# Modulation weights of the feed-forward stages: scaled and summed on DVE and POOL instead of multiplied on PE

## The chip, the cores and the metric

The kernel runs on one core of a Trainium2 chip. The metric is the device time of one execution in microseconds. Five engines take part: PE (matmuls; PEld is its weight load), DVE and ACT (elementwise work), POOL (elementwise work, here also the triangular inverses), and SP, whose queue issues nearly all DMA transfers.

## The reference, cut to what matters

One inference step of a diffusion backbone with two layers. Each layer has a feed-forward half step, a stage of token mixing, and a second feed-forward half step; ahead of each stands a norm whose shift, scale and gate come from conditioning vectors.

```python
def modulation(cond, w_mod, b_mod):
    m = jax.nn.silu(cond) @ w_mod + b_mod
    return m.reshape(cond.shape[0], N_MOD, D_MODEL)      # N_MOD = 9, D_MODEL = 1024

def adaln(x, g, shift, scale):
    return rms_norm(x, g) * (1.0 + scale) + shift

def swiglu(h, w_in, w_out):
    gate, up = jnp.split(h @ w_in, 2, axis=-1)           # w_in 1024 x 5632, w_out 2816 x 1024
    return (jax.nn.silu(gate) * up) @ w_out
```

There are two conditioning vectors (context tokens and latent tokens), so the product with `w_mod` (1024 x 9216 in each layer) has two rows of input. 128 context tokens and 128 latent tokens go through the same weights.

## The kernel before

Activations lie channel-major: 128 channels on the partitions, 8 chunks of channels, 256 tokens in a row. Weights are fp32 and stream through SBUF in tiles `raw` of 128 x 1024 (three buffers). Half a tile at a time is split into two parts that sum to it, `hi` on ACT and `lo = raw - hi` on DVE (four buffers each, `split`, lines 155 and 158), and every pair of a 128 x 128 weight block and a chunk of activations takes three matmuls on PE: `hi` with the high and the low part of the activations, `lo` with the high part.

`ffn` is run four times, and is called here the first to the fourth feed-forward stage. It loops over 11 pairs of column blocks: `pg` (gate) and `pu` (up) are 48 matmuls each, out of eight halves of weight tiles; ACT, DVE and DVE again make `z` out of them, which is split into `zhi` and `zlo`. Then five output units `po` follow (three of 256 columns, two of 128), whose result is added to `xT` on DVE. After a stage comes the next norm (`adaln`, with `rstd`: `pss`, `nr`, `prs`, `u`, `hhi`, `hlo`).

A modulation vector is 1024 columns of `w_mod`, in eight row chunks `mraw` of 128 x 1024. `mod_part` makes eight loads and eight products of it, and a last step. A product is four matmuls with the chunk of the conditioning vectors `cT` (2 of 32 columns used) as the stationary operand, into four groups of partitions of one PSUM tile `acc`; the profile counts two records for each of these fp32 matmuls. The last step copies `acc` to `modrow` on ACT, transposes it with two matmuls (`acct`) and adds the bias on DVE (`mod`). Of the 18 vectors two are done at the start, six in the first feed-forward stage, four each in the second and third, and one in each mixing stage. `fill` emits loads and products up to counts that grow with the blocks of the stage; in the first three stages the last 18 steps (`KEEP`) are left to `flush`, which emits them in the following norm. A list scheduler then sets the order on each engine by priorities and its own estimates; every engine and SP's queue work strictly in that order.

Of the kernel before, what the change touches and what calls it, by code (L numbers as in the profile page):

```python
# [10 lines left out]
F32 = mybir.dt.float32  # L11
# [4 lines left out]
ALU = mybir.AluOpType  # L16
# [8 lines left out]
OUT_UNITS = ((0, 2), (2, 2), (4, 2), (6, 1), (7, 1))      # first chunk and number of chunks of the output products  # L25
# [4 lines left out]
# column offsets of w_in  # L30
# [3 lines left out]
def constants():  # L34
    """Tables that depend on shapes alone, packed along the free dimension."""
# [28 lines left out]
    for d in range(2):  # L64
        for l in (16, 8, 4, 2, 1):
            tt = (t16 // l) * 2 * l + t16 % l + (l if d == 0 else 0)      # token of a compact index
            su = (si % (2 * l)) >= l
            ms.append(f((si // (2 * l) == tt // (2 * l)) & (su if d else ~su)))
# [29 lines left out]
KEEP = (18, 18, 18, 0)  # L98
MRAW, NQ = 16, 15


class Net:
    def __init__(self, ctx, tc, ia, oa, dbg=None):
# [13 lines left out]
        self.ch = 0                 # which of the two chains of small products is being written  # L117
# [63 lines left out]
    def after(self, later, earlier):  # L181
        """issue order of two instructions of one queue"""
        self.tc.add_manual_dep(later.ins, earlier.ins.name,
                               mybir.DependencyInfo(mybir.DependencyClass.NoSync, mybir.DependencyReason.DATA),
                               reason="issue order")
# [12 lines left out]
    def wload(self, srcs, nk, nc_):  # L198
        """srcs: list of (column offset in tile, dram view [128, nk, n])."""
# [7 lines left out]
        def part(k0, n):  # L207
            """rows k0 .. k0 + n as two f32r parts that sum to them"""
# [10 lines left out]
    def gemm(self, out2, wview, nkc, xhi, xlo, ncol=256, segs=None):  # L219
        """out2: psum tile [128, 512] -> (2, 256) column chunks; weights  # L220
        stationary, channel-major activations moving."""
# [23 lines left out]
    def params_g(self):  # L245
        """conditioning vectors and modulation biases first, the small parameters later"""
# [40 lines left out]
    def mod_part(self, tiles, l, v):  # L287
        """a modulation vector (1024 columns) as loads and products, a pair per weight tile, and a
        last step. Column groups of 256 in the four column tiles of the PE array."""
# [19 lines left out]

        def last():  # L310
            row = self.sm.tile([128, 256], F32, tag="mrow", name="modrow", bufs=2)
# [4 lines left out]
            # chunk of the vector = j * 2 + c  # L316
# [6 lines left out]
        return [partial(load, k) for k in range(8)], [partial(prod, k) for k in range(8)] + [last]  # L323

    def queue(self, parts):
        """modulation work for the rest of the sublayer"""
# [5 lines left out]
        tiles = lambda: [pool.tile([128, 1024], F32, tag="mraw", name="mraw", bufs=MRAW)]  # L332
        for p in parts:
            x, y = self.mod_part(tiles, *p)
# [3 lines left out]
    def fill(self, nload, nprod):  # L338
        """the queued loads and products up to these counts, the loads never too few"""
# [5 lines left out]
    def flush(self):  # L345
        """what is left, in the shadow of a norm"""
# [5 lines left out]
    def modcols(self, l, i):  # L352
        """per-sublayer columns: g * (1 + scale), shift, gate factor."""
# [13 lines left out]
    def rsqrt(self, p, n, scale, eps):  # L367
        """(p * scale + eps)^-1/2 of [128, n]: a first guess from the exponent, then three
        Newton steps (the sign alternates)"""
# [10 lines left out]
    def rstd(self):  # L380
        """[128, 256] psum: 1 / rms of every token, on all partitions"""
# [21 lines left out]
    def headnorm(self, x, n, scale, eps):  # L403
        """(sum over each 64-partition group of x^2 * scale + eps)^-1/2: psum tiles of 512 columns of x"""
# [20 lines left out]
    def adaln(self, l, i):  # L425
        """x * g (1 + scale) ahead of the norm factor, which comes last; at the start the
        other way round, as the modulation comes last there"""
# [32 lines left out]
    def ffn(self, l, w, i):  # L460
        """the modulation parts are spread over the products; the last steps (keep) wait for the next norm"""
# [39 lines left out]
    # SBUF of this phase is shared by tag: tiles of one tag have disjoint lives.  # L501
# [29 lines left out]
    def padded(self, p):  # L531
        """[128, (2 chunks, 2 streams, 128)] psum -> sbuf with a zero column at each end"""
# [43 lines left out]
    def proj_gate(self, c0, nm):  # L576
        """x * (1 + tanh(x / 2)): silu without its factor 1/2, which is in the norm weights"""
# [8 lines left out]
    def proj_t(self, l):  # L586
        """token-major: values of B and D, the scalar gates of C"""
# [33 lines left out]
    def proj_d(self, l):  # L621
        """q with the heads in the order 0, 2 | 1, 3, and k"""
# [833 lines left out]
```

## Time and profile before

| | |
|---|---|
| median of three runs | 1675.52 us (1665.06 to 1677.17) |
| span of the profiled execution | 1665.8 us |
| busy: PE, DVE, ACT, POOL | 1620.0, 1057.8, 811.3, 143.7 us |
| feed-forward stages one to four, products only | 218.1, 203.2, 201.2, 189.0 us |
| mean granted clock of TensorE | 0.979 |

No time of the profiled execution is listed beside its span. A busy time is the time in which at least one instruction of the engine was under way. The stretch of a stage is taken from its first `pg` matmul to its last `po` matmul.

### The profile page before, as it was taken

What the parts mean: (1) busy time and instruction counts of PE and PEld (TensorE: products, weight loads), DVE (VectorE), ACT (ScalarE), POOL (GpSimd) and SP (SyncE); (2) the same over time, 40 slices, a digit from 0 to 9 for tenths busy, and PEclk for the clock granted to TensorE, in tenths of its full rate; (3) what the DMA queues carried; (4) which work ended last, traced back from release to release, by engine and by line L of the source; (5) the groups of instructions that cost most, each with busy time, mean ns of one, the idle gap of its engine ahead of it and who ended that gap; (6) DMA issues with size and microseconds to landing.
All of it is one profiled execution on the core that took longest, in us unless ns stands there. A gap on an engine that the chain in (4) does not pass through costs nothing.

```text
span 1665.8 us, 34996 instructions
## 1 busy us (share of the span) xinstructions
PE 1620.0 (97%) x13862; PEld 1465.2 (88%) x13872; DVE 1057.8 (64%) x2270; ACT 811.3 (49%) x1529; POOL 143.7 (9%) x304
## 2 busy tenths in 40 slices
PE   6999999999999999999999999999999999999997
PEld 3999988788778998999989999887887899989997
DVE  4555557667687477665566655674857774866655
ACT  3444445446444455454455545551744443655553
POOL 0000000043007000000000000000700350000000
PEclk9999999999999999999999999998989998999999
DMA  9998775344246455976669766551423563645553
GB/s 342 315 318 297 238 238 164 80 117 114 64 132 199 127 173 195 324 266 221 213 228 316 245 213 211 189 139 48 122 74 95 158 195 95 187 143 182 186 184 121
DMA packets 300821, 311.14 MB, mean 187 GB/s; under 512 B 48368, under 2 KB 278768, under 8 KB 300656
## 3 DMA queue, kind: packets, MB, share of 16 engines
q1 hardware_dynamic: 300368, 307.85, 58.2%
q8 instruction: 109, 1.79, 0.4%
q10 hardware_dynamic: 288, 1.05, 0.2%
q14 instruction: 56, 0.46, 0.1%
HBM read 303.87 MB, written 4.98 MB: 185 GB/s over the span
## 4 chain that ended last, share of the span: by engine, by line
PE 75%; DVE 4%; POOL 2%; DMA 2%; ACT 2%; issue 1%; SPq 0%; POOLq 0%; DVEq 0%; ACTq 0%
PE pg L170 20%; PE po L170 15%; PE pu L170 13%; PE wk L170 6%; PE sv L170 4%; PE pA L170 3%; PE acc L170 3%; PE pC L170 1%; PE pD L170 1%; PE yA L170 1%; PE pR L170 1%; PE pT L170 1%; POOL itmp L842 1%; POOL Tb L843 1%; DVE lo L158 1%
## 5 line engine op out<-in xcount | busy, mean ns | idle before, releaser
L158 DVE TENSOR_TENSOR lo<-raw,hi 128x512 fp32r<-128x512 f32 (+2 forms) x840 | 581.0, 696 | 394.0 <-ACT hi L155 381.8
L155 ACT ACTIVATE hi<-raw 128x512 fp32r<-128x512 f32 (+2 forms) x840 | 523.2, 626 | 592.4 <-PE pg L170 192.3
L170 PE MATMUL pg<-hhi,hi 128*128 128x256 f32 x1216 | 356.5, 293 | 6.0 <-ACT hi L155 2.9
L170 PE MATMUL pg<-hlo,hi 128*128 128x256 f32 x1216 | 352.8, 290 | 0.5 <-DVE hlo L158 0.3
L170 PE MATMUL pg<-hhi,lo 128*128 128x256 f32 x1216 | 349.7, 288 | 0.8 <-DVE lo L158 0.6
L170 PEld LDWEIGHTS pg<-hhi,hi 128*128 128x128 f32 x1216 | 236.0, 194 | 23.6 <-issue 8.8
L170 PEld LDWEIGHTS pg<-hlo,hi 128*128 128x128 f32 x1216 | 236.1, 194 | 7.7 <-issue 4.4
L170 PEld LDWEIGHTS pg<-hhi,lo 128*128 128x128 f32 x1216 | 236.7, 195 | 3.1 <-DVE lo L158 2.3
L170 PE MATMUL pu<-hhi,lo 128*128 128x256 f32 x704 | 199.3, 283 | 0.0
L170 PE MATMUL pu<-hlo,hi 128*128 128x256 f32 x704 | 199.2, 283 | 0.0
L170 PE MATMUL pu<-hhi,hi 128*128 128x256 f32 x704 | 199.2, 283 | 0.0
L170 PE MATMUL po<-zhi,hi 128*128 128x256 f32 x704 | 198.6, 282 | 0.0
L170 PE MATMUL po<-zhi,lo 128*128 128x256 f32 x704 | 196.8, 280 | 0.0
L170 PE MATMUL po<-zlo,hi 128*128 128x256 f32 x704 | 196.7, 279 | 0.0
L170 PEld LDWEIGHTS po<-zhi,hi 128*128 128x128 f32 x704 | 132.6, 188 | 6.2 <-issue 4.5
L170 PEld LDWEIGHTS pu<-hhi,lo 128*128 128x128 f32 x704 | 135.2, 192 | 0.1
L170 PEld LDWEIGHTS pu<-hhi,hi 128*128 128x128 f32 x704 | 135.2, 192 | 0.0
L170 PEld LDWEIGHTS pu<-hlo,hi 128*128 128x128 f32 x704 | 135.2, 192 | 0.0
L170 PEld LDWEIGHTS po<-zhi,lo 128*128 128x128 f32 x704 | 132.9, 189 | 0.0
L170 PEld LDWEIGHTS po<-zlo,hi 128*128 128x128 f32 x704 | 132.5, 188 | 0.0
L170 PE MATMUL acc<-mraw,cT 128*32 128x256 f32 x1152 | 85.7, 403 | 9.6 <-DMA mraw<-in_w_mod 9.5
L191 POOL COPY GB<-SA 32x128 f32<-32x128 f32 x16 | 5.7, 355 | 911.2 <-DMA out_o_v<-VD 584.6
(354 smaller groups left out, 2610.6 us busy)
## 6 DMA issues: line engine op xcount, KB each, us to landing
raw<-in_ffn_w_in SPq DMA_DIRECT2D x176, 512.0 KB, 4.5
mraw<-in_w_mod SPq DMA_DIRECT2D x138, 512.0 KB, 5.7
raw<-in_w_in SPq DMA_DIRECT2D x106, 512.0 KB, 3.6
raw<-in_ffn_w_out SPq DMA_DIRECT2D x76, 512.0 KB, 4.4
raw<-in_w_branch SPq DMA_DIRECT2D x32, 256.0 KB, 3.2
raw<-in_w_out SPq DMA_DIRECT2D x16, 512.0 KB, 4.1
raw<-in_ffn_w_out SPq DMA_DIRECT2D x12, 256.0 KB, 3.0
raw<-in_ffn_w_out SPq DMA_DIRECT2D x8, 384.0 KB, 4.4
```

Source lines behind the costliest of these rows:

```text
L155: self.nc.scalar.activation(out, in_, func, bias=bias, scale=scale, **kw)
L158: self.nc.vector.tensor_tensor(out, a, b, op)
L170: self.nc.tensor.matmul(out, lhsT, rhs, start=start, stop=stop)
L191: (self.nc.vector if eng == "v" else self.nc.gpsimd).tensor_copy(out, in_)
L842: nc.gpsimd.tensor_tensor(tv, a, b, ALU.mult)
L843: nc.gpsimd.tensor_tensor(T[:, 0:n, j + 1:32], T[:, 0:n, j + 1:32], tv, ALU.subtract)
```

## The change

In the three feed-forward stages that carry modulation work, a chunk of weights no longer goes to PE. Each chunk is multiplied with the two conditioning values of its rows (a scalar for each partition) and added to two running sums `macc` of 128 x 1024, one for each conditioning vector: the second sum on DVE with one instruction a chunk, the first on POOL with two, of which the first overwrites the chunk. When all eight chunks are added, PE sums the 128 rows of both with a matmul against a column of ones (`sel`), into the same layout as before, and the last step goes on as it was. The two vectors at the start and the two of the mixing stages keep their products. `KEEP` falls from 18 to 1, the buffers of `mraw` from 16 to 10, and four buffers `macc` are added.

```diff
-KEEP = (18, 18, 18, 0)
-MRAW, NQ = 16, 15
+KEEP = (1, 1, 1, 0)
+MRAW, MACC, NQ = 10, 4, 15
...
+        self.sel = self.cp.tile([128, 2, 32], F32, name="sel")
+        nc.gpsimd.memset(self.sel, 0.0)
+        for e in range(2):
+            nc.gpsimd.memset(self.sel[:, e, e:e + 1], 1.0)
...
-    def mod_part(self, tiles, l, v):
+    def mod_part(self, tiles, l, v, sums=None):
...
+        def fold(k):
+            raw, = raws.pop(k)
+            if k == 0:
+                acc.extend([sums(), sums()])
+            c0, c1 = [self.cT[:, k, e:e + 1] for e in range(2)]
+            if k == 0:
+                self.ts(acc[1], raw, c1, None, ALU.mult)
+                self.nc.gpsimd.tensor_scalar(acc[0], raw, c0, None, ALU.mult)
+            else:
+                self.stt(acc[1], raw, c1, acc[1], ALU.mult, ALU.add)
+                self.nc.gpsimd.tensor_scalar(raw, raw, c0, None, ALU.mult)
+                self.nc.gpsimd.tensor_tensor(acc[0], acc[0], raw, ALU.add)
+
+        def rows():
+            p = self.py.tile([128, 256], F32, tag="y", name="acc")
+            for e in range(2):
+                for j in range(4):
+                    self.mm(p[32 * j:32 * j + 32], self.sel[:, e], acc[e][:, 256 * j:256 * j + 256], e == 0, e == 1)
+            acc[:] = [p]
+
         def last():
+            if sums:
+                rows()
...
-        return [partial(load, k) for k in range(8)], [partial(prod, k) for k in range(8)] + [last]
+        step = fold if sums else prod
+        return [partial(load, k) for k in range(8)], [partial(step, k) for k in range(8)] + [last]
...
-        tiles = lambda: [pool.tile([128, 1024], F32, tag="mraw", name="mraw", bufs=MRAW)]
+        tiles = lambda: [pool.tile([128, 1024], F32, tag="mraw", name="mraw", bufs=MRAW if fold else 16)]
+        sums = lambda: pool.tile([128, 1024], F32, tag="macc", name="macc", bufs=MACC)
...
-        net.queue([(0, 0), (0, 1)])
+        net.queue([(0, 0), (0, 1)], False)
```

On DVE, early in the first stage, the stream before has only the residuals and the work on `z`:

```order
L158 TENSOR_TENSOR zlo<-z,zhi 128x512
L158 TENSOR_TENSOR lo<-raw,hi 128x512 x4
L161 SCALAR_TENSOR_TENSOR z<-z,pg 128x512
L158 TENSOR_TENSOR lo<-raw,hi 128x512 x3
L158 TENSOR_TENSOR z<-z,pu 128x512
```

and after the change the sums stand among them, one by one or up to three in a row:

```order
L161 SCALAR_TENSOR_TENSOR z<-z,pg 128x512
L161 SCALAR_TENSOR_TENSOR macc<-mraw,cT,macc 128x1024 x3
L158 TENSOR_TENSOR z<-z,pu 128x512
L158 TENSOR_TENSOR lo<-raw,hi 128x512 x2
L158 TENSOR_TENSOR zlo<-z,zhi 128x512
L158 TENSOR_TENSOR lo<-raw,hi 128x512 x4
L161 SCALAR_TENSOR_TENSOR macc<-mraw,cT,macc 128x1024
L158 TENSOR_TENSOR lo<-raw,hi 128x512 x2
```

What moved: nothing of the old work; 112 instructions of 1024 columns were put in between.

POOL, which had no work in these stages, now has the following from the first chunk of the first vector on (the tile numbers tell the chunks apart; DMAHW is a transfer, and a wait for DVE is one for DVE's reading of the chunk):

```order
L324 TENSOR_SCALAR macc_496<-mraw_490,cT_102 128x1024 [waits DMAHW1_49,DVE_49]
L327 TENSOR_SCALAR mraw_492<-mraw_492,cT_102 128x1024 [waits DMAHW2_49,DVE_49]
L328 TENSOR_TENSOR macc_496<-macc_496,mraw_492 128x1024 [waits Pool_49]
L327 TENSOR_SCALAR mraw_494<-mraw_494,cT_102 128x1024 [waits DMAHW4_49,DVE_49]
L328 TENSOR_TENSOR macc_496<-macc_496,mraw_494 128x1024 [waits Pool_49]
```

Each chunk is scaled in place once DVE has read it, and then added.

On PE, in the second stage, between the first blocks, one step of products stood before:

```order
L170 MATMUL pu<-hlo,hi 128x256
L170 MATMUL pu<-hhi,lo 128x256
L170 MATMUL acc<-mraw,cT 32x256 x4
L170 MATMUL pg<-hhi,hi 128x256
L170 MATMUL pg<-hlo,hi 128x256
```

and after the change, where a vector's eight chunks are complete, the row sums and seven weight matmuls later the transposes:

```order
L170 MATMUL pu<-hhi,lo 128x256
L170 MATMUL acc<-macc,sel 32x256 x8
L170 MATMUL pg<-hhi,hi 128x256
L170 MATMUL pg<-hlo,hi 128x256
L170 MATMUL pg<-hhi,lo 128x256
L170 MATMUL pg<-hhi,hi 128x256
L170 MATMUL pg<-hlo,hi 128x256
L170 MATMUL pg<-hhi,lo 128x256
L170 MATMUL pg<-hhi,hi 128x256
L175 MATMUL acct<-cst,modrow 128x128 x2
```

The steps between most blocks are gone, and PE now waits at these places for POOL's last addition.

## Rows read from the trace of the kernel before

**Rows 1.** Windows of the four stages: length, busy us (count) by engine, clock, DMA, GB/s.
```profile
30.90:249.00 218.10, 214.37 (x1849) 200.28 (x1850) 126.06 (x225) 106.91 (x188) 0.00 (x0) 0.98 0.84 282
640.40:843.60 203.20, 202.70 (x1720) 193.21 (x1724) 123.09 (x217) 103.43 (x183) 0.00 (x0) 1.00 0.75 249
855.40:1056.60 201.20, 201.20 (x1726) 192.98 (x1726) 120.40 (x208) 102.09 (x175) 0.00 (x0) 1.00 0.76 251
1463.90:1652.90 189.00, 188.78 (x1571) 187.84 (x1572) 119.55 (x202) 101.94 (x177) 0.00 (x0) 1.00 0.55 171
```
**Rows 2.** The first window for instructions with `acc` alone: PE, PEld, ACT.
```profile
30.90:249.00 218.10, 18.71 (x257) 7.01 (x258) 1.49 (x4) 0.98 0.84 282
```
**Rows 3.** Chain of waits, second and fourth stage: start us, us, what.
```profile
661.03 5.76 PE pu L170 x48
666.79 0.57 PE acc L170 x8
...
673.30 5.76 PE pu L170 x48
...
1477.23 5.76 PE pg L170 x48
...
1488.75 5.76 PE pg L170 x48
```
**Rows 4.** DVE's groups in the second stage: count, busy us, mean ns, idle before.
```profile
L158 DVE TENSOR_TENSOR lo<-raw,hi 128x512 fp32r<-128x512 f32 x131 | 90.1, 691 | 74.4 <-ACT hi L155 70.1 <-PE pu L170 1.6 <-PE po L170 1.3
L158 DVE TENSOR_TENSOR z<-z,pu 128x512 f32<-128x512 f32 x11 | 7.6, 687 | 3.2 <-PE pu L170 3.2
L161 DVE SCALAR_TENSOR_TENSOR xT<-po,ga,xT 128x128 f32<-128x128 f32 x16 | 4.6, 344 | 0.3 <-PE po L170 0.3
```
**Rows 5.** Timeline of DVE, without POOL (658) and beside POOL (363 to 369).
```profile
658.60 2.49 DVE L158 TENSOR_TENSOR lo<-raw,hi 128x512 fp32r<-128x512 f32 x4
...
363.86 0.89 DVE L158 TENSOR_TENSOR lo<-raw,hi 128x512 fp32r<-128x512 f32 x1
365.52 3.42 DVE L158 TENSOR_TENSOR lo<-raw,hi 128x512 fp32r<-128x512 f32 x4
369.25 0.69 DVE L161 SCALAR_TENSOR_TENSOR SRB<-SRB,pR 128x512 f32<-128x512 f32 x1 [0.31 <-ACT SRB L155]
```
**Rows 6.** Timeline of PE at the end of the first stage: idle time before in brackets.
```profile
240.10 0.69 PE L175 MATMUL acct<-cst,modrow 128*128 128x128 f32 x2 [3.21 <-ACT modrow L155]
...
241.02 0.41 PE L170 MATMUL po<-zlo,hi 128*128 128x256 f32 x1
241.23 0.41 PE L170 MATMUL po<-zhi,lo 128*128 128x256 f32 x1
```
**Rows 7.** Chain of waits in the norm after the second stage.
```profile
851.07 0.39 ACT modrow L155
...
851.51 0.44 PE acct L175 x2
851.95 3.59 PE acc L170 x64
```
**Rows 8.** Timeline of POOL in the first mixing stage.
```profile
321.59 1.27 POOL L191 COPY GB<-SA 32x128 f32<-32x128 f32 x4 [5.22 <-ACT SA L155]
328.73 0.52 POOL L831 MEMSET Tb<- 128x512 f32 x1 [5.87 <-DVE BK L161]
352.27 0.25 POOL L843 TENSOR_TENSOR Tb<-Tb,itmp 128x31 f32<-128x31 f32 x1
359.55 0.42 POOL L843 TENSOR_TENSOR Tb<-Tb,itmp 128x115 f32<-128x115 f32 x1
365.96 0.77 POOL L843 TENSOR_TENSOR Tb<-Tb,itmp 128x133 f32<-128x133 f32 x1
369.30 0.46 POOL L843 TENSOR_TENSOR Tb<-Tb,itmp 128x136 f32<-128x136 f32 x1
```
**Rows 9.** Window behind PE's stop in the first stage: length, PE busy (count), clock, DMA, GB/s.
```profile
240.40:242.90 2.50, 2.50 (x13) 0.50 0.66 202
```

More of the change, by code (lines that the diff above doesn't have):

```diff
@@ L321, in last, with queue @@
                 self.tt(o[:, :, :, e:e + 1], x[:, :, :, e:e + 1], b, ALU.add)
-        return [partial(load, k) for k in range(8)], [partial(prod, k) for k in range(8)] + [last]
-    def queue(self, parts):
+        step = fold if sums else prod
+        return [partial(load, k) for k in range(8)], [partial(step, k) for k in range(8)] + [last]
+    def queue(self, parts, fold=True):
         self.mr = ExitStack()
@@ L331, in queue @@
         pool = self.mr.enter_context(self.tc.tile_pool(name="mr", bufs=1))
-        tiles = lambda: [pool.tile([128, 1024], F32, tag="mraw", name="mraw", bufs=MRAW)]
+        tiles = lambda: [pool.tile([128, 1024], F32, tag="mraw", name="mraw", bufs=MRAW if fold else 16)]
+        sums = lambda: pool.tile([128, 1024], F32, tag="macc", name="macc", bufs=MACC)
         for p in parts:
-            x, y = self.mod_part(tiles, *p)
+            x, y = self.mod_part(tiles, *p, sums if fold else None)
             self.loads += x + [lambda: None]
```

## The prediction

> **What bounds the kernel now.** I read first the busy times by stage, one stretch for each feed-forward product stage [rows 1]. In all four PE is busy for the whole stretch (202.7 of 203.2 us in the second) at the full granted clock (0.98 to 1.00), while DVE is busy for 120 to 126 us and POOL not at all. The last stage has no modulation work and lasts 189.0 us; the first three last 218.1, 203.2 and 201.2. So the surplus over the last is 29, 14 and 12 us, and in the first of them the modulation matmuls are busy for 18.7 us [rows 2]. The chain of waits shows the same as a rhythm [rows 3]: in the second stage one pair of a `pg` and a `pu` group returns after 12.27 us (661.03 to 673.30), in the last after 11.52 us (1477.23 to 1488.75). The difference of 0.75 us is one step of eight `acc` records with its change-over. PE is the bound, and what the change takes from it is on the path.
>
> DVE has the second place. Of its rows in the second stage the residual `lo` (131 at 0.69 us) is the largest [rows 4]. Back to back four take 2.49 us, that is 0.60 us from one to the next [rows 5].
>
> **What is removed, and its worth.** In the three stages every step of 4 matmuls on a weight chunk goes. Up to the 189.0 us of the last stage this gives 29 + 14 + 12 = 55 us. Of the first stage's 29 us some 4 are a stop of PE on a transpose that waits for ACT, and the stretch of low clock behind it [rows 6]. What stays on PE is, for each of 14 vectors, one group of eight row-sum matmuls and two transposes, two steps of 0.75 us by [rows 3] with the change of operand: 10 to 21 us in all. So the relief of PE is worth 55 - 15 = 40 us at most inside the stages. At each of the three norms that follow, 64 records of `acc` stand for 3.6 us on the chain ahead of the next products [rows 7]; with them gone the next limit is DVE's own `hlo` work. I take 0 to 3 us at each norm, 5 in all. If nothing else became late, the change would be worth 45 us.
>
> **What is added.** For each of 14 x 8 chunks (48 in the first stage, 32 in the second and in the third): on DVE one scalar_tensor_tensor of 1024 columns (for the first chunk of a vector a tensor_scalar), and on POOL one tensor_scalar and, except for the first, one tensor_tensor of 1024 columns.
>
> DVE: the 512-column form is spaced by 0.60 us; 512 more columns at the slope of two lengths (128 columns 0.34, 512 columns 0.69 us [rows 4], so 0.9 to 1.0 ns a column; I take 1.04 as the upper value) make 1.13 us. The first-chunk form I take at 0.6. The sum for the first stage is 42 x 1.13 + 6 x 0.6 = 51 us, for the other two 28 x 1.13 + 4 x 0.6 = 34 us each. DVE alone would then be busy for some 177 us of the first stage, and 157 of the second, still below PE.
>
> POOL: the trace has no operation of this length there, so I extend it. An unhindered tensor_tensor takes 0.25 us at 31 columns and 0.42 at 115 [rows 8], that is 2.0 ns a column, so 1024 columns stream for 1.9 to 2.1 us. A tensor_scalar has one tensor to read. The nearest rows are the memset of 512 columns in 0.52 us and four copies of 128 columns in 1.27 us [rows 8], so 1.0 us for 1024 columns; its bounds are half of the tensor_tensor (0.95) and all of it (2.1). One chunk then holds POOL for h = 7/8 x 2.0 + 1.0 = 2.75 us (2.6 to 2.9, and 3.9 with the dear tensor_scalar). The Trainium skill (GPSIMD Engine Reference, Engine selection) has a one-input operation on POOL roughly at line rate; at one column a cycle of the 1.2 GHz that the page gives, a tensor_scalar would be an estimated 0.85 us and the first stage below 262 instead of 269 us. No row here shows one.
>
> **The two engines hold each other up.** This is the step that decides. In the stretch where POOL works on its triangular systems beside DVE, a `lo` takes 0.89 instead of 0.69 us, and four of them 3.42 instead of 2.49 us [rows 4, 5]; POOL's tensor_tensor of 133 columns takes 0.77 us, where 136 columns unhindered take 0.46 [rows 8]. One DVE and one POOL operation alternate with a period of (3.42 - 0.91) / 3 = 0.84 us, which is DVE's 0.60 plus the 0.24 us that 126 columns on POOL need. So the two do not run side by side there: their times add. Where DVE reads one operand from PSUM, POOL is not held: beside `SRB` its 136 columns take 0.46 us [rows 5, 8].
>
> So I add the times of the operations that exclude each other, for each stage. DVE's share now: 132 `lo` and 11 `zlo` at 0.60, 86 us. First stage: 86 + 51 + 48 x 2.75 = 269 us, against the present 218.1: 51 us longer. Second and third: 86 + 34 + 32 x 2.75 = 208 us, against 203.2 and 201.2: 5 and 7 us longer. PE with its 189 us and the row sums lies below in all three and has no say.
>
> To this comes what is not hidden. DVE's 22 operations on `z` with a PSUM operand (at 0.60) and its 16 residual updates (4.6 us) are 18 us of each stage [rows 4]: free if POOL streams beside all of them, all paid if beside none. POOL streams in a half of the time (132 of 269), so I pay half, 9 us in each stage, 27 in all. And each vector now ends in a chain over four engines: the last POOL addition, eight row sums on PE, the copy `modrow` on ACT, two transposes on PE, two additions on DVE. In the instruction streams all of these stand ahead of weight work on their engine: behind the row sums on PE the next `pg` group, behind `modrow` on ACT the next `hi`, behind the additions on DVE the next `lo`. From `modrow` to the end of the transposes the present chain takes 0.9 us [rows 7]; with the row sums and the additions some 1.7. POOL may be at the next vector's chunks meanwhile, so I count a part, 0.5 us for 14 vectors, 7 us (0 to 24).
>
> The DMA requests are the same in number and order; the weight tiles for modulation are 10 instead of 16, and POOL now frees them. Behind a load that waits for a tile on SP's queue stand the loads of the feed-forward weights. It costs nothing while POOL is less than some seven chunks (19 us) behind; where it is more, it only passes the same delay on.
>
> **The sum:** 51 + 5 + 7 + 27 + 7 - 5 = 92 us on the profiled execution's span of 1665.8. I lower it to 80 us, since the 0.84 us period holds POOL's short operation at its low bound (1.9 ns a column), with which h is 2.6 and the stages shrink by 7, 5 and 5 us, of which I take the larger part. The runs shown lie between 1665.06 and 1677.17 us, with the median 9.7 above the span; I add the 80 us to the median and forecast 1755 us.
>
> The bounds: with h = 2.6, every PSUM operation hidden, no chain cost and 9 us gained at the norms, 44 + 0 + 2 - 9 = 37 us, 1713. With h = 3.9 and the 18 us unhidden in each stage: 137 + 187 + 18 = 342 for the first and 120 + 125 + 18 = 263 for the others, 246 us in all; this needs a tensor_scalar as slow as a tensor_tensor, which the copies speak against.
>
> **Rivals.**
> (a) POOL's long streams do not hold DVE as the short ones do: it hinders DVE at the start of an operation only. Then PE stays the bound in all stages and 45 us are gained, 1630. For it: the rows show only POOL operations of up to 136 columns, where a start cost and a hold cannot be told apart well. Against it: what DVE is late by (0.24 us) is the streaming time of POOL's columns at 1.9 ns each, not a fixed amount. Its point of decision is the hold of a chunk: below (189 + 8 - 137) / 48 = 1.25 us in the first stage and (193 - 120) / 32 = 2.3 us in the others PE is the bound again. The Trainium skill (SBUF — State Buffer, Who interferes with whom) says that a DVE operation with two SBUF inputs and a POOL operation that reads SBUF share one read port, which the first holds for its whole length. By that rule rival (a) is out and the forecast's sum stands; the trace agrees in the short case (0.89 against 0.69 us), and none of its rows has a long one.
> (b) The hold is real but shorter, about 2.0 us a chunk: then the first stage takes 137 + 96 = 233, 15 us longer, the others 193 and 8 to 10 us less, and the time is the same within 1%, 1675.
> (c) PE waits at the row sums long enough that its clock falls. Ahead of 240.1 us PE stood for 3.2 us, and afterwards its matmuls came 0.21 us apart (241.02, 241.23) instead of 0.12 [rows 6], with a granted clock of 0.50, the lower level of 1.2 GHz [rows 9]. If each of 14 vectors brings a stop of 3 us (one chunk of POOL) and 12 matmuls at half speed (1.1 us) that the adding-up above does not cover, the time is 1755 + 14 x 4.1 = 1812. For it: the last chunks of a stage come in bursts of three or four. Against it: PE has slack of 70 us in the first stage.
>
> **Chances.** The forecast with its bounds 0.66, (c) 0.12, (a) 0.12, (b) 0.10. A difference of 1% is about what a measurement of this kernel can tell from no change (its three runs differ by 0.7%). So faster 0.12, same 0.10, slower 0.78. The range leaves out (a) and the dear end of the costs: 1670 to 1830.
>
> **What would show it.** In the first stage after the change: `lo` at a mean well above 0.69 us and up to 2.5 us, POOL's tensor_tensor at 2 us and more, PE waiting for DVE `lo`; a stage of 260 to 290 us, and the others 205 to 225. The last stage and both mixing stages stay as they are. The prediction is wrong if `lo` stays at 0.69 us beside POOL's long operations, or if a tensor_scalar on POOL takes far less than 0.9 us.

## The result, and the profile after

The changed kernel takes 1839.53 us (median of four, 1835.26 to 1855.02) beside 1670.29 for the kernel before (1664.28 to 1677.17): a ratio of 1.112, 95% interval 1.101 to 1.123. The forecast was 1755 us with a range to 1830. The direction was right, and the loss is twice what was forecast. Runs of one kernel lie up to 3% apart, the longer ones at a lower granted clock, and for five kernels below (scaling left out, addition left out, DVE's share left out, the first with folds held late, and the last) the profiled run is one of the longer, so that in their traces DVE's and POOL's busy times say more than lengths.

The page of the profile after: busy times, and for four engines and the granted clock the busy tenths of 40 slices of the span.

```profile
span 1840.3 us, 34171 instructions
PE 1633.6 (89%) x13200; PEld 1484.6 (81%) x13200; DVE 1404.1 (76%) x2382; ACT 803.2 (44%) x1529; POOL 813.7 (44%) x517
PE   6586688799999999877899778899999999999998
DVE  5989798676767647999977999967657776676655
POOL 0999999204302400799942999900060043000000
PEclk9889889799999989989998999999989999999999
```

Where POOL shows 9, in the three stages with modulation work, PE has fallen to 5 to 8 and DVE stands at 7 to 9. From first `pg` to last `po`, and from there to the next stage, the two traces give:

| | before | after | difference |
|---|---|---|---|
| first stage | 217.8 | 296.8 | +79.0 |
| to the second | 391.7 | 405.2 | +13.5 |
| second stage | 202.8 | 250.2 | +47.4 |
| to the third | 12.2 | 8.0 | -4.2 |
| third stage | 200.8 | 249.2 | +48.4 |
| to the fourth | 407.7 | 397.7 | -10.0 |

That is 174.1 of the 174.5 us between the spans. The fourth stage is 190.4 us in both; the 189.0 us that the prediction took for it end 1.4 us before its last `po` matmul, so that the first three stages exceed it by 50 us and not by 55. The windows after, each stage cut where the `pg` and `pu` blocks end and the output products begin [rows 1], first and second stage:

```profile
core 0: us, PE busy (x) PEld busy (x) DVE busy (x) ACT busy (x) POOL busy (x), PEclk, DMA share, GB/s
31.00:243.50 212.50, 152.25 (x1127) 142.19 (x1127) 189.76 (x187) 73.26 (x130) 196.13 (x61) 0.88 0.61 210
243.50:327.90 84.40, 71.76 (x552) 69.62 (x548) 77.93 (x88) 31.81 (x57) 83.40 (x28) 0.92 0.60 194
733.00:919.00 186.00, 146.62 (x1091) 137.21 (x1092) 182.35 (x179) 68.55 (x125) 170.74 (x53) 0.95 0.62 210
919.00:983.30 64.30, 63.88 (x549) 62.96 (x548) 45.85 (x73) 33.05 (x58) 21.74 (x8) 1.00 0.58 180
```

In the second stage the whole loss lies in the blocks. DVE is busy for 182.35 of their 186 us, and PE for 147. Beside the output products PE is again busy throughout and DVE for 45.85 of 64.3 us. The same blocks before took 137.6 us with DVE busy for 84.9, the output products 65.2.

DVE's groups in these blocks [rows 4]:

```profile
L158 DVE TENSOR_TENSOR lo<-raw,hi 128x512 fp32r<-128x512 f32 x87 | 100.1, 1179 | 3.0 <-ACT hi L155 3.0
L161 DVE SCALAR_TENSOR_TENSOR macc<-mraw,cT,macc 128x1024 f32<-128x1024 f32 x28 | 56.3, 2010 | 0.0
L158 DVE TENSOR_TENSOR z<-z,pu 128x512 f32<-128x512 f32 x10 | 6.7, 674 | 0.0
```

A `lo` has grown from 0.69 to 1.18 us, while `z`, with one operand in PSUM, is as short as before. The 28 sums in these blocks and 4 first chunks, which are a tensor_scalar on DVE, are all 32 chunks of the stage; POOL is later, with 24 of its 28 additions in the blocks and 4 beside the output products. The two longest of POOL's groups over the three stages, minimum, median and maximum in ns:

```profile
L327 POOL TENSOR_SCALAR mraw<-mraw,cT x98: 2837/3798/4376, 46.3 to 1186.3; 128x1024 f32<-128x1024 f32 x98
L328 POOL TENSOR_TENSOR macc<-macc,mraw x98: 2337/2722/3505, 50.1 to 1190.2; 128x1024 f32<-128x1024 f32 x98
```

The addition (L328) was priced at 2.0 us and takes 2.34 at the least; the scaling (L327) was priced at 1.0 and never takes less than 2.84. A stretch of the second stage on DVE, then on POOL [rows 5, 8]; the columns are start and duration:

```profile
759.68 2.88 DVE L158 TENSOR_TENSOR lo<-raw,hi 128x512 fp32r<-128x512 f32 x1
762.48 0.68 DVE L158 TENSOR_TENSOR z<-z,pu 128x512 f32<-128x512 f32 x1
763.08 1.00 DVE L158 TENSOR_TENSOR lo<-raw,hi 128x512 fp32r<-128x512 f32 x1
764.01 0.68 DVE L158 TENSOR_TENSOR zlo<-z,zhi 128x512 fp32r<-128x512 f32 x1
764.61 0.68 DVE L158 TENSOR_TENSOR lo<-raw,hi 128x512 fp32r<-128x512 f32 x1
```

```profile
759.29 2.72 POOL L328 TENSOR_TENSOR macc<-macc,mraw 128x1024 f32<-128x1024 f32 x1
761.99 3.29 POOL L327 TENSOR_SCALAR mraw<-mraw,cT 128x1024 f32<-128x1024 f32 x1
765.36 3.35 POOL L328 TENSOR_TENSOR macc<-macc,mraw 128x1024 f32<-128x1024 f32 x1
```

The `lo` that starts while an addition runs ends 0.55 us after it (762.56 against 762.01): it stood until the addition was over. Beside the scaling from 761.99 to 765.28 four DVE operations run, three of them at 0.68 us and one late by 0.3. So a scaling is long but hardly holds DVE. Last, PE's waits in the first stage, and DVE's longest:

```profile
PE acc L170 <- POOL macc L328: 27.7, 3, 14.4
PE pu L170 <- DVE lo L158: 20.2, 13, 2.9
PE pg L170 <- DVE lo L158: 15.4, 7, 6.5
```

```profile
DVE mod L158 <- PE acct L175: 20.9, 3, 11.5
```

The columns are us in all, times, and the longest. Three row sums waited 27.7 us for POOL's last addition, and one more behind the stage waited some 7.6 us (327.86 to 335.44). DVE stood for 20.9 us at the `mod` additions that come behind these row sums.

What PE was to be relieved of is gone. In the first stage its work on `acc` falls from 18.71 [rows 2] to 7.95 us:

```profile
31.00:327.90 296.90, 7.95 (x80) 2.62 (x80) 1.90 (x5) 0.89 0.60 205
```

In the norm after the second stage the 3.59 us of `acc` records [rows 7] no longer stand on the chain of waits; DVE's work, `prs` and `hhi` follow each other up to the next products:

```profile
988.84 1.23 PE prs L170 x4
990.07 0.02 issue
990.09 0.43 DVE u L158
990.53 0.02 issue
990.55 0.70 ACT hhi L155 x2
991.25 0.04 issue
991.29 1.04 PE pg L170 x2
```

### The profile page after: what moved, and what is told of

It reads as the page before. It is cut to its first block, busy times and chain, and to the rows that moved or that the text cites. A ratio compares the mean times of both kernels' runs of the same rounds, so it can differ in the third digit from the quotient of the medians.

```text
span 1840.3 us, 34171 instructions
## 1 busy us (share of the span) xinstructions
PE 1633.6 (89%) x13200; PEld 1484.6 (81%) x13200; DVE 1404.1 (76%) x2382; ACT 803.2 (44%) x1529; POOL 813.7 (44%) x517
## 4 chain that ended last, share of the span: by engine, by line
PE 38%; DVE 8%; issue 3%; DMA 2%; ACT 1%; DVEq 0%; SPq 0%; ACTq 0%
PE po L170 11%; PE pg L170 9%; PE pu L170 6%; DVE lo L158 3%; PE wk L170 3%; DVE macc L161 2%; PE pA L170 2%; DMA raw<-in_ffn_w_in 1%; PE sv L170 1%; PE pD L170 1%; PE pC L170 1%; PE yA L170 1%; ACT hi L155 0%; PE pT L170 0%; PE phr L170 0%
## 5 line engine op out<-in xcount | busy, mean ns | idle before, releaser
L158 DVE TENSOR_TENSOR lo<-raw,hi 128x512 fp32r<-128x512 f32 (+2 forms) x840 | 728.0, 881 | 208.6 <-ACT hi L155 203.9
L170 PE MATMUL pg<-hhi,lo 128*128 128x256 f32 x1216 | 358.4, 295 | 47.7 <-DVE lo L158 47.0
L327 POOL TENSOR_SCALAR mraw<-mraw,cT 128x1024 f32<-128x1024 f32 x98 | 361.7, 3691 | 21.3 <-DVE macc L161 21.3
L170 PE MATMUL pg<-hlo,hi 128*128 128x256 f32 x1216 | 357.5, 294 | 0.5 <-DVE hlo L158 0.3
L328 POOL TENSOR_TENSOR macc<-macc,mraw 128x1024 f32<-128x1024 f32 x98 | 265.7, 2711 | 7.9
L170 PE MATMUL pu<-hhi,lo 128*128 128x256 f32 x704 | 209.3, 297 | 56.5 <-DVE lo L158 56.2
L170 PEld LDWEIGHTS pg<-hhi,hi 128*128 128x128 f32 x1216 | 241.0, 198 | 17.0 <-ACT th L155 4.4
L170 PEld LDWEIGHTS pg<-hlo,hi 128*128 128x128 f32 x1216 | 240.9, 198 | 7.1 <-issue 3.6
L161 DVE SCALAR_TENSOR_TENSOR macc<-mraw,cT,macc 128x1024 f32<-128x1024 f32 x98 | 191.0, 1949 | 0.6 <-DMA mraw<-in_w_mod 0.4
```

Of the source, the lines that this page charges most:

```text
L158: self.nc.vector.tensor_tensor(out, a, b, op)
L161: self.nc.vector.scalar_tensor_tensor(out, a, s, b, op0, op1)
L170: self.nc.tensor.matmul(out, lhsT, rhs, start=start, stop=stop)
L327: self.nc.gpsimd.tensor_scalar(raw, raw, c0, None, ALU.mult)
L328: self.nc.gpsimd.tensor_tensor(acc[0], acc[0], raw, ALU.add)
```

## The experiments

In the expectations of the four runs that were made first (scaling left out, addition left out, memsets, both sums on DVE) theory L is the forecast's own (POOL's reading operations hold DVE up) and theory P says that POOL's own length is the limit. In the later ones S is the forecast's theory as a sum on DVE, and L a rival in which the length of a single hold counts. Each ratio is to runs of the kernel before on the same chip, with its 95% interval.

**Scaling left out.** POOL only adds the unscaled chunks 2 to 8 (the first sums are wrong by that).

```diff
-                self.nc.gpsimd.tensor_scalar(raw, raw, c0, None, ALU.mult)
                 self.nc.gpsimd.tensor_tensor(acc[0], acc[0], raw, ALU.add)
```

> Left out: POOL's scaling of chunks 2 to 8 (the unscaled chunk is added). POOL has 2.7 us a chunk instead of 6.4. Theory L: the additions still hold DVE for 2.2 us each, so in the block part of the second stage DVE's 105 us plus 26 x 2.2 = 57 us make 162 instead of 186 us, and the whole about 1755 us. Theory P: POOL is never the bound, about 1640 us.

**Addition left out.** The other half of POOL's work alone; the first sum is only the first chunk.

```diff
                 self.nc.gpsimd.tensor_scalar(raw, raw, c0, None, ALU.mult)
-                self.nc.gpsimd.tensor_tensor(acc[0], acc[0], raw, ALU.add)
```

> Left out: POOL's additions; the scalings in place stay (2.84 us unhindered). If a scaling holds DVE's port only for the 0.84 us by which a lo behind it is late, the block part of the second stage has 105 + 29 x 0.84 = 129 us on DVE and PE is the bound again: about 1640 us. If it holds the port for its whole length, 105 + 29 x 2.84 = 187 us, and about 1840 us. Theory P: 29 x 2.9 = 84 us, about 1640 us.

Additions alone: 1823.82 us (1806.74 and 1840.89; the second is the profiled one), at the lower value 143 us above the kernel before on that chip (1663.68). Scalings alone: 1673.50, ratio 1.005 (1.000 to 1.010). Blocks and output products of the second stage, first with additions alone, then with scalings alone:

```profile
736.60:920.20 183.60, 150.96 (x1093) 143.56 (x1094) 177.35 (x179) 68.76 (x124) 92.21 (x32) 0.91 0.62 213
```

```profile
660.10:801.00 140.90, 134.54 (x1092) 129.27 (x1093) 131.86 (x179) 68.40 (x124) 110.78 (x32) 1.00 0.81 277
801.00:864.60 63.60, 63.60 (x547) 62.84 (x546) 37.49 (x73) 33.04 (x58) 0.00 (x0) 1.00 0.59 182
```

With additions alone POOL is idle for half of the blocks and they stay long, with DVE busy for 177.35 of 183.6 us; that is against theory P. But the gain that L expected did not come either: without scalings DVE's busy time falls by only 5 us, from 182.35 to 177.35. With scalings alone POOL is busier (110.78), DVE is at 131.86, and PE is busy for 134.5 of 140.9 us. Most of the loss hangs on the additions.

**POOL busy without reading.** Memsets of the same tiles in place of scaling and addition (the first sums are then zero). The first chunk, not shown, gets three memsets of its sum.

```diff
...
-                self.nc.gpsimd.tensor_scalar(raw, raw, c0, None, ALU.mult)
-                self.nc.gpsimd.tensor_tensor(acc[0], acc[0], raw, ALU.add)
+                for _ in range(3):
+                    self.nc.gpsimd.memset(raw, 0.0)
+                for _ in range(3):
+                    self.nc.gpsimd.memset(acc[0], 0.0)
```

> Left out: the sums of the first conditioning vector; POOL fills the same tiles with zeros instead, six memsets of 1024 columns a chunk (about 6.2 us at the 0.52 us of 512 columns), behind the same waits. So POOL is as busy as after the change (6.4 us a chunk) but reads nothing from SBUF. Theory L (POOL's reading holds DVE's second operand, and DVE so lengthened sets the pace): the block parts fall to PE's pace, lo at 0.69 us, about 1640 us. Theory P (POOL's own time for a chunk sets the pace, handed on by the row sums and by the weight tiles that it frees): nothing gained, 1800 to 1840 us.

It took 1812.91 us, ratio 1.088 (1.077 to 1.100), as P had it, but not by P's way: in the blocks of the second stage `lo` stayed at 0.69 us beside memsets, and over the three stages DVE stood still twelve times for 10.6 to 23.6 us, each time behind a tensor_scalar. So the first chunk's tensor_scalar on DVE was replaced:

```diff
-                self.ts(acc[1], raw, c1, None, ALU.mult)
+                self.stt(acc[1], raw, c1, raw, ALU.mult, ALU.add)
```

> The kernel with six memsets of 1024 columns a chunk on POOL in place of scaling and addition, and the first chunk of a vector on DVE as a scalar_tensor_tensor (raw times its column plus raw, so that the sums are wrong) instead of a tensor_scalar. In the run with memsets DVE stood still 12 times for 10.6 to 23.6 us behind a tensor_scalar with its operands in SBUF, 184 us in all; in 8 of them, 126 us, it was the first chunk's. Theory M (the memsets cost nothing as such; what stood still was DVE's tensor_scalar, which waited for a pause of POOL): 1813 - 126 = 1687 us (1670 to 1705), with four stops left at the two other places. Theory P (a POOL that is busy all the time is the limit by itself): 1790 or more, with DVE waiting at other instructions.

1742.49 us, ratio 1.048 (1.042 to 1.054). The eight stops at first chunks are gone; five of 12.4 to 38.1 us are left, all at the other tensor_scalars (`ga` and `u`), and they are longer than M reckoned with. One of them on DVE, what POOL did as it began and as it ended, and the window of the blocks of the second stage, into which no stop fell:

```profile
1042.18 37.59 DVE L165 TENSOR_SCALAR ga<-mod 128x16 f32<-128x16 f32 x1
1042.26 37.52 DVE L158 TENSOR_TENSOR lo<-raw,hi 128x512 fp32r<-128x512 f32 x1
```

```profile
1041.26 0.95 POOL L325 MEMSET macc<- 128x1024 f32 x1
1042.16 0.94 POOL L329 MEMSET mraw<- 128x1024 f32 x1
1043.06 0.95 POOL L325 MEMSET macc<- 128x1024 f32 x1
...
1077.91 0.94 POOL L329 MEMSET mraw<- 128x1024 f32 x1
1078.80 2.97 POOL L331 MEMSET macc<- 128x1024 f32 x3
```

```profile
699.10:837.90 138.80, 133.03 (x1093) 130.16 (x1094) 118.91 (x179) 69.27 (x124) 128.64 (x144) 0.99 0.82 282
```

POOL is busy for 128.64 of 138.80 us there, all sums of DVE stand in the same blocks, and they take 138.8 us, as before the change (137.6). So a POOL that is busy does not lengthen the blocks by that, and DVE's own time with 32 chunks is 118.9 us. (Four of them are here a scalar_tensor_tensor of 1.28 us in place of a tensor_scalar of 0.75, which makes this base some 2 us too high.) Against it the additions alone add 177.35 - 118.91 = 58.4 us, 2.09 for each of 28; the scalings alone add 13.0 us, 0.40 for each of 32 (0.47 with the lower base); both together add 63.4 us, 1.98 a chunk. What no run here reaches is POOL without holds at its own pace: at its shortest times 28 x (2.84 + 2.34) + 4 x 2.84 = 156 us, an estimate that lies above the 138.8 us, so POOL would be the next limit.

**Both sums on DVE**, so that POOL has no part; nothing is left out.

```diff
-                self.nc.gpsimd.tensor_scalar(acc[0], raw, c0, None, ALU.mult)
+                self.ts(acc[0], raw, c0, None, ALU.mult)
...
-                self.nc.gpsimd.tensor_scalar(raw, raw, c0, None, ALU.mult)
-                self.nc.gpsimd.tensor_tensor(acc[0], acc[0], raw, ALU.add)
+                self.stt(acc[0], raw, c0, acc[0], ALU.mult, ALU.add)
```

> Both sums on DVE, two scalar_tensor_tensor of 1.13 to 1.2 us a chunk, POOL has nothing; nothing left out. Theory L: nothing holds DVE, its own sum in the block parts is about 72 + 29 x 2.3 = 139 us (35 chunks and 152 us in the first stage), just above PE's 127 to 138, so 1640 to 1665 us, at or a little below the kernel before. Theory P says the same, since POOL is out. If DVE itself, without any hold, is too slow, the time stays above 1700 us.

1671.16 us, ratio 1.000 (0.995 to 1.005). The blocks of the second stage take 138.8 us with DVE busy for 131.3, the stage 202.4; the first stage, with six vectors, takes 233.5. A second instruction of 1.28 us on DVE costs less than two on POOL. The relief of PE, sized at 40 us within the stages, is not seen: PE is busy for 134.3 us of these blocks, against 137.1 before and 128.2 in the blocks of the last stage.

**DVE's share left out**, the row sums read POOL's sum twice (the second conditioning vector gets the first one's modulation).

```diff
-                acc.extend([sums(), sums()])
+                acc.extend([sums()] * 2)
...
-                self.ts(acc[1], raw, c1, None, ALU.mult)
...
-                self.stt(acc[1], raw, c1, acc[1], ALU.mult, ALU.add)
```

> The kernel after without DVE's share: POOL alone scales and sums, for one of the two batch entries, and the row sums read that sum twice (the other batch entry gets the wrong modulation). Theory S: DVE's work in the blocks of the second stage falls from 182 to 128 - 39 + 28 x 2.1 = 148 us, the blocks take about 150 and the stage 215; the first stage is then POOL's own, 48 chunks at 5.2 to 5.6 us, 250 to 268; in all 1715 to 1735. Theory L: the holds are as many and as long, and each stops PE as before: above 1790. If POOL's own pace in company (6.2 us a chunk) is the limit of the first stage whatever DVE does, that stage stays at 300 us and the time is about 1765.

1757.70 us, ratio 1.054 (1.047 to 1.062), and by stages 275.9, 212.4 and 218.7. The blocks of the second:

```profile
726.50:872.80 146.30, 134.15 (x1093) 130.30 (x1094) 120.75 (x145) 68.14 (x124) 133.55 (x44) 0.97 0.77 265
```

Their length is near the 150 us that S expected, but not for S's reason: DVE is busy for 120.75 us of them and not for 148, less than PE and POOL, and only 20 of the 28 additions fall into them. So this run does not test the sum on DVE. The first stage was sized too small: POOL is busy for 261.1 of its 275.9 us, DVE for 183.4. Forty-eight chunks at 5.4 us are a second limit there, close under the first.

**Additions in halves:**

```diff
-                self.nc.gpsimd.tensor_tensor(acc[0], acc[0], raw, ALU.add)
+                for c in (slice(0, 512), slice(512, 1024)):
+                    self.nc.gpsimd.tensor_tensor(acc[0][:, c], acc[0][:, c], raw[:, c], ALU.add)
```

> The kernel after, with each addition on POOL in two of 512 columns. Theory S: the sum of the holds is the same (2 x 1.1 us), so 1825 to 1855, with lo behind a half at about 1.8 us instead of 2.85 and twice as many of them. Theory L: a hold of 1.1 us fits into PE's lead, so the stops fall by more than half and the time is 1760 or less.

1835.02 us, ratio 1.107 (1.100 to 1.114): the time does not change. In the blocks of its second stage:

```profile
L158 DVE TENSOR_TENSOR lo<-raw,hi x86: 677/684/1783, 752.4 to 921.6; 128x512 fp32r<-128x512 f32 x86
```

No `lo` takes more than 1.78 us there now, and the gain that L expected did not come. The holds are not quite the same in sum, as S had it: DVE is busy for 214.9 us of the second stage instead of 228.2, and the stage takes 239.3. The first is some 12 us longer, with 47.3 us of PE's waits at row sums instead of 27.7.

**Row sums four chunks later**, for PE's waits on POOL.

```diff
-            self.loads += x + [lambda: None]
-            self.prods += y
+            for steps, new in ((self.loads, x + [lambda: None]), (self.prods, y)):
+                held = steps.pop() if steps and fold else None
+                steps += new
+                if held:
+                    steps.insert(len(steps) - len(new) + 4, held)
```

> The kernel after, with the row sums, the copy, the transposes and the additions of a vector put four chunks later, behind the fourth chunk of the next vector. If PE's waits at the row sums (35 us in four waits in the first stage of the kernel after) are a part of the loss, the first stage falls from 297 to 260 to 270 us and the time to 1805. If POOL's own pace sets the end of the first stage (it is busy for 287 of its 306 us), that stage stays at 285 us or more, and the time at 1825 to 1845. The second and third stage stay at 250 us by both.

1823.08 us, ratio 1.097 (1.086 to 1.109). PE's wait at row sums up to the end of the first stage falls to 1.1 us, and the stage only from 296.8 to 288.1. What limits it then is DVE, busy for 279.6 of 288.1 us; POOL is busy for 271.6. The second and third, expected at 250, take 241.8 and 244.6, with 28 of 32 chunks beside the blocks. The second, blocks and output products:

```profile
721.50:891.00 169.50, 142.84 (x1093) 134.61 (x1094) 167.98 (x172) 68.36 (x124) 154.66 (x48) 0.97 0.66 227
891.00:963.00 72.00, 65.69 (x545) 62.98 (x544) 56.65 (x80) 31.02 (x58) 39.27 (x13) 0.98 0.54 167
```

Four chunks that moved out of the blocks made them 16.5 us shorter (DVE is again busy for 99%) and the output products only 8 us longer: work does cost less there.

**Folds held late** in the second and third stage: 22 chunks beside the blocks and 10 beside the output products, each sum on DVE ordered behind the instruction of DVE that the program emits just before it, and loads of chunks issued at most three ahead; and the same with row sums four chunks later.

```diff
+LATE = [0, 0, 3, 5, 8, 10, 13, 15, 18, 21, 24, 27, 30, 32, 34, 35, 36]
...
+            self.fill(min(nl, LATE[p] + 3), LATE[p])
...
+            prev = self.lastv
...
                 self.stt(acc[1], raw, c1, acc[1], ALU.mult, ALU.add)
+                if self.held:
+                    self.after(self.lastv, prev)
```

> The kernel after, but in the second and third stage 22 chunks are folded beside the eleven pg/pu blocks and 10 beside the output products, where the kernel after folds all 32 beside the blocks. Theory S (DVE is the bound, and its own time and the holds of POOL's additions add up within a part of a stage, so that a part with too many folds is long and the other part gives nothing back): the two parts of a stage together hold 182 + 46 = 228 us of DVE work, so each of the two stages takes about 230 us instead of 251, and the time is 1798 us (1785 to 1810). Theory L (a single hold of 2.2 us is longer than PE's lead of some four pairs of weight tiles; what counts is the number of holds and their length, not where they stand): unchanged, 1835 to 1850.

> The late folds of the earlier kernel (22 chunks beside the blocks, 10 beside the output products in the second and third stage) together with row sums four chunks later. That earlier kernel's stages of 268.6 and 266.3 us held stops of PE at the row sums of some 13 us each. Theory S (DVE's sum, 182 + 46 us, is the bound, wherever folds stand): 228 to 235 us for each of the two stages, and 1795 us with the first as in the kernel after (1765 if that too is shorter). Theory that the late place itself costs as much as it gives back: 250 us or more for each, and 1835 or above.

1912.43 us, ratio 1.146 (1.138 to 1.155), and 1870.09, ratio 1.127 (1.118 to 1.135). Both miss what S expected. In the first, PE stood at four row sums of the second stage and the norm behind it for 44.5 us, waiting for POOL, and DVE stood with it, since the `mod` additions that need the row sums came next in its queue. In the second kernel the second stage still takes 249.5 us; its blocks, ACT's longest wait in them, and a wait of SP's queue (line 307 is the load of a chunk, line 335 POOL's addition):

```profile
742.00:916.60 174.60, 142.77 (x1093) 135.41 (x1094) 142.15 (x168) 67.93 (x123) 130.12 (x40) 0.95 0.64 212
```

```profile
ACT hi L157 <- DMA raw<-in_ffn_w_in: 48.5, 16, 8.1
```

```profile
SPq L307 <- POOL macc L335: 60.5, 11, 8.9
```

DVE is no longer full (142 of 175 us). ACT waits 48.5 us for weight tiles instead of 18.5. The trace shows why for the longest of these waits: a load of a chunk stands on SP's queue until POOL's addition frees its tile, and the loads of the feed-forward weights stand behind it. POOL's addition ends at 840.46, the load of the chunk goes out at 840.50, the load of `raw` at 840.93, and ACT starts on it at 845.98, after 6.07 us of waiting; three waits of 7.0 to 8.1 us go the same way. In the kernel after SP's queue waits for POOL for less than 1 us in these blocks. So a fold moved out of the blocks gave its time back to DVE, but with POOL behind, the weight loads came late.

**First stage as before, the others on DVE alone**, once with folds held late as above and once in the scheduler's own order.

```diff
-KEEP = (1, 1, 1, 0)
+KEEP = (18, 1, 1, 0)
...
-        self.queue(PARTS[f])
+        self.queue(PARTS[f], f > 0)
...
-                self.nc.gpsimd.tensor_scalar(raw, raw, c0, None, ALU.mult)
-                self.nc.gpsimd.tensor_tensor(acc[0], acc[0], raw, ALU.add)
+                self.stt(acc[0], raw, c0, acc[0], ALU.mult, ALU.add)
```

> First stage as in the kernel before (chunks on PE); in the second and third stage both sums of each chunk on DVE and none on POOL, 22 chunks beside the blocks and 10 beside the output products; row sums and norms as in the kernel after. Theory S: DVE has 112 us in the 130 us of the blocks and 64 in the 65 us of the output products, so PE bounds both stages at 195 to 200 us (before 203 and 201), and the norms are shorter by 4.6 and 4.1: 1650 us (1643 to 1658). If DVE's folds of 2.56 us a chunk delay lo whatever the slack, the gain is lost as when all 14 vectors were on DVE: 1663 to 1672.

> First stage on PE as in the kernel before; second and third stage with both sums on DVE, in the order that the compiler's scheduler gives them, not held late. With all 14 vectors on DVE the first stage took 233.5 us and the others 202.4 and 202.0; with the first at 217.8 again the time is 16 us below that kernel, 1655 (1648 to 1662), a gain of 0.5%. If the gain at the norms is lost elsewhere: 1663 to 1672. If the order held late was not what made the previous attempt slow: 1690.

Held late: 1695.88 us, ratio 1.022 (1.017 to 1.026), second and third stage 221.1 and 218.8. In the scheduler's order: 1650.17 us, ratio 0.991 (0.986 to 0.995), stages 202.7 and 198.1. In the second stage 45 of 64 instructions on chunks stand beside the blocks in the one and 47 of 65 in the other, so it is not where they stand but how they are held there that costs 18 to 21 us a stage; which part of that edit does it, the order on DVE or the loads issued only three chunks ahead, no run separates. The last kernel is the fastest of all, 0.9% below the kernel before.

## Why the prediction was wrong in size

| term of the sum | forecast | measured |
|---|---|---|
| first stage | 51 + 9 + 3 = 63 | 79.0 |
| second stage | 5 + 9 + 2 = 16 | 47.4 |
| third stage | 7 + 9 + 2 = 18 | 48.4 |
| norms, and what lies between stages | -5 | -0.7 |
| in all | 92, lowered to 80 | 174.1 |

**The mechanism was right for the additions.** DVE's time and that of POOL's additions add. Scalings alone cost 0.5% (0.0 to 1.0), additions alone most of the loss (143 us at the least, of 169), both sums on DVE nothing. The Trainium skill (SBUF — State Buffer, Who interferes with whom) has DVE operations with two SBUF inputs and POOL operations that read SBUF exclude each other for the whole operation. The additions agree (2.09 us of 2.34 and more), the scalings, which read SBUF too, do not (0.40 of 2.84 and more).

**The failed step is "So I add the times of the operations that exclude each other, for each stage".** It spreads a stage's work over all of its length. The second stage has DVE work of 182.35 + 45.85 = 228.2 us, but all 32 chunks fall into the blocks, which DVE fills by itself (98%), and 18.5 us of DVE's time beside the output products stay unused, where PE sets the pace. With 3.7 us of idle time in the blocks that is 22 of the 33 us between the forecast's sum (86 + 34 + 88 + 9 = 217 us) and the stage of 250.2. The row sums put later bear this out: with four chunks beside the output products the stage is 8.4 us shorter. Whether some order of the folds reaches the 228 us is open: those that were tried did not.

**The remaining 11 us are two mis-sized terms of opposite sign.** The holds, forecast as 32 x 2.75 = 88 us, are 228.2 - 156.4 = 71.8: the addition's hold was priced about right (2.0, measured 2.09), the scaling's at 1.0 instead of 0.40. DVE's own time was counted as 86 + 34 + 9 = 129 us and is 156.4 (118.9 in the blocks, 37.5 beside the output products where POOL is idle). The forecast took only what excludes POOL, and half of the operations with a PSUM operand; but once DVE is the bound, all that it does counts. The prediction had the figure ("DVE alone would then be busy for some 177 us of the first stage, and 157 of the second") and left it out of the sum.

**In the first stage the sum came near by luck, and the waits of rival (c) came on top.** 269 + 9 = 278 us were forecast, and DVE is busy for 267.7, but by the same two errors: by the prediction's own 177 us the holds are some 91 us and not 132. Of the other 29 us of 296.8 DVE stands for 20.9 at the `mod` additions behind the late row sums: the chain over four engines, counted at 3 us for this stage. "PE has slack of 70 us in the first stage" was no argument against these waits, since DVE, the bound, stands with PE. Row sums put later gave back only 9 us of them, since DVE's busy time rose from 267.7 to 279.6 us with the same chunks: 12.0 us of POOL's additions had run while DVE stood, and only 3.1 do so in that run. (c)'s other half, the fall of PE's clock, is not shown to have cost anything. POOL is busy for 94% of that shorter stage and nearly a limit as well. That comes from the scaling's own length, which lies outside the forecast's bounds (0.95 to 2.1 us).

**The other rivals.** The condition of (b), a hold of about 2.0 us a chunk, came true in the blocks (1.98) and its time, 1675, did not: it used the same whole-stage sum without DVE's other work. (a) fell with the first `lo` of 2.88 us. Lowering 92 to 80 by the short period had no ground in the long operations. The tiles that POOL frees on SP's queue, put at nothing, did cost nothing here; they came in only where the folds were held late. Between first and second stage 7.6 of the 13.5 us are the last row sum; the others stay open, since this stretch also takes 396.8 and 402.0 us in the two kernels whose first stage is that of before. The 10.0 us gained between third and fourth stay open too. The way from second to third stage is 4.2 us shorter, where 0 to 3 were forecast for a norm.

## What to carry to other kernels

Before work goes to a second engine, add up all that the busier of the two does in the part of the stage where the scheduler puts the new work, not over the whole stage; the idle time of a part that another engine bounds does not help the other part. If a slower engine then frees the tiles of a shared load queue, look at what stands behind its loads. Between DVE and POOL the form of the instruction decides: an addition of two SBUF tensors on POOL took nearly its whole length from DVE, so one fused instruction on DVE (1.28 us) was cheaper than two on POOL. Price an instruction by a row of its own kind: the scaling's price came from memsets and copies and was off by a factor of nearly three.

## What the hardware showed that was not expected

On POOL a tensor_scalar with a scalar for each partition took at least 2.84 us for 128 x 1024 in fp32, more than a tensor_tensor (2.34), and yet held DVE for only 0.40 to 0.47 us; DVE takes 0.75 us for the same.

A DVE tensor_scalar on SBUF operands, even one of 128 x 16, did not get in among back-to-back memsets on POOL: in the case shown it stood for 37.6 us, some forty memsets of 0.94 us, until POOL paused for 0.06 us (1079.74 to 1079.80, within the three memsets from 1078.80). In the blocks without a stop scalar_tensor_tensor (1.28 us) and `lo` (0.69 us) went on at full speed beside the same memsets. The Trainium skill (SBUF — State Buffer, Who interferes with whom) says of tensor_scalar that it can take the shared pair of ports and that the second to issue waits until the first operation is finished; here it waited for many operations, not for one.
